# Rotating a matrix by 90 degrees: taller macro tiles, row chunks that come free one by one, and narrow macro tiles at both ends

## The chip, the cores and the metric

The kernel runs on one core of a Trainium2 chip. The metric is device time in microseconds (us), lower is better. The core has 16 DMA engines, a TensorE (PE), a VectorE (DVE), a ScalarE (ACT), and a sequencer (SP) that issues the reads here; ACT issues the writes.

## The reference

```python
def setup_inputs():
    return {"x": np.random.randn(8192, 8192).astype(np.float32), "k": 1}

def reference(x, k):
    return np.rot90(x, k)
```

There is no arithmetic to speak of: 268.4 MB are read, 268.4 MB are written. A rotation is a transpose with the order of the rows reversed.

## The kernel before

A macro tile is 512 rows by 4096 columns. Each 128-row strip is read as one DMA of 2 MB with runs of 16 KB (tile `a`), DVE copies it with every block of 128 columns reversed (`ar`), PE transposes 128x128 blocks into PSUM, ACT copies PSUM to an output tile of 1 MB (`o`), and ACT issues its write. A row of an output block is 512 floats, so each piece in memory is 2 KB.

```python
R = 512; C = 4096; RT = R // P; CG = C // P; G = 2048 // R; PW = 2048 // R
a_pool: bufs=2      r_pool: bufs=2 * RT      o_pool: bufs=5      psum: bufs=2
for r0 in range(0, N, R):
    for c0 in range(0, M, C):
        for t in range(RT):
            a = a_pool.tile([P, C], dt, tag="a")
            nc.sync.dma_start(out=a[:], in_=x[r0 + t * P : r0 + (t + 1) * P, c0 : c0 + C])
            ar = r_pool.tile([P, C], dt, tag="ar")
            nc.vector.tensor_copy(...)            # reversed within each 128 columns
        for g0 in range(0, CG, G):
            o = o_pool.tile([P, G, R], dt, tag="o")
            ...                                   # 16 transposes into ps, then:
            nc.scalar.copy(o[:, G - PW - h : G - h, :], ps[:])
            nc.scalar.dma_start(out=dst, in_=o[:])   # 128 x 4 pieces of 512 floats
```

## Time and profile before

Before: 1280.81 us median of 4 runs (1279.27 to 1282.25). Four lines of the page: DMA busy share and rate in 40 slices, and the two lines of the chain that ended last.

```profile
DMA  9999999999999999999999999999999999999998
GB/s 364 424 425 424 426 423 424 426 425 424 424 425 427 422 426 424 424 426 426 422 422 425 422 425 424 422 422 424 427 417 427 420 423 426 417 428 421 425 422 352
DMA 91%; PE 4%; ACT 3%; issue 0%; DVE 0%; ACTq 0%; SPq 0%
DMA out_dram<-o 90%; PE ps L96 4%; ACT o L101 3%; DMA a<-in_x_dram 2%; DVE ar L83 0%; ACTq L107 0%; ACTq L101 0%; SPq L77 0%
```

Between the ends the DMA engines are never idle: only their rate, and the two ends, can be improved. GB/s counts what is read and what is written together. The windows view gives, per stretch, its length, busy time of PE, PEld, DVE, ACT and POOL, the granted clock, the DMA busy share and GB/s.

```profile
0.00:170.00 170.00, 86.00 (x480) 76.57 (x480) 45.70 (x20) 53.39 (x29) 0.70 (x6) 0.73 1.00 414
170.00:1116.00 946.00, 535.31 (x3072) 486.56 (x3072) 215.82 (x95) 358.39 (x192) 0.00 (x0) 0.72 1.01 424
1116.00:1278.20 162.20, 86.74 (x544) 78.20 (x544) 29.64 (x13) 67.18 (x36) 0.00 (x0) 0.77 0.98 410
```

Two lines of the waits view, 170 to 1116 us (waiter <- releaser: us in total, times, longest):

```profile
ACT o L101 <- DMA out_dram<-o: 548.3, 159, 6.9
DVE ar L83 <- PE ps L96: 370.0, 25, 21.2
```

And the beginning, where only reads run (timeline: start us, duration, what; in brackets the idle time before and its releaser):

```profile
8.01 2.29 DVE L83 COPY ar<-a 128x4096 f32<-128x4096 f32 x1 [8.01 <-DMA a<-in_x_dram]
12.87 2.29 DVE L83 COPY ar<-a 128x4096 f32<-128x4096 f32 x1 [2.57 <-DMA a<-in_x_dram]
18.92 2.29 DVE L83 COPY ar<-a 128x4096 f32<-128x4096 f32 x1 [3.76 <-DMA a<-in_x_dram]
24.41 2.29 DVE L83 COPY ar<-a 128x4096 f32<-128x4096 f32 x1 [3.19 <-DMA a<-in_x_dram]
```

Strips of 2 MB come 4.9 us apart at first and then 5.5 to 6.1 us apart. With two `a` buffers at most two reads are in flight, and that is not enough to keep the rate when nothing is written beside them (tested in e8 and e13 below).

### The profile page before, as it was taken

How to read it: one execution, taken by the hardware profiler on the slowest of the kernel's cores; microseconds unless marked ns; L12 is line 12 of the kernel's file. 1: busy time of each engine (PE TensorE's matmuls, PEld its weight loads, DVE VectorE, ACT ScalarE, POOL GpSimd, SP SyncE). 2: the span in 40 equal slices, each digit the busy share in tenths (PEclk: the TensorE clock that was granted, in tenths of full speed). 3: DMA queues.
4: the chain of work that ended last, by engine and by line, in shares of the span. 5: the costliest groups of instructions: out<-in, count | busy, mean ns of one | idle time of the engine just before them, and what ended most of it. 6: DMA issues, size and time to landing. Idle time of an engine off the chain costs nothing.

```text
span 1278.2 us, 9636 instructions
## 1 busy us (share of the span) xinstructions
PE 708.0 (55%) x4096; PEld 641.3 (50%) x4096; DVE 291.2 (23%) x128; ACT 479.0 (37%) x257; POOL 0.7 (0%) x6
## 2 busy tenths in 40 slices
PE   2546565555545656546555465555565645656464
PEld 1545554455544545545554455554554534546453
DVE  3322222122221221212222122221222221222210
ACT  1324443343432434324343344342343432534354
POOL 0000000000000000000000000000000000000000
PEclk9757675777877777667686767777767776777788
DMA  9999999999999999999999999999999999999998
GB/s 364 424 425 424 426 423 424 426 425 424 424 425 427 422 426 424 424 426 426 422 422 425 422 425 424 422 422 424 427 417 427 420 423 426 417 428 421 425 422 352
DMA packets 55339, 537.51 MB, mean 421 GB/s; under 512 B 6144, under 2 KB 6144, under 8 KB 6144
## 3 DMA queue, kind: packets, MB, share of 16 engines
q10 hardware_dynamic: 36864, 268.45, 50.5%
q1 hardware_dynamic: 18432, 268.44, 49.6%
q8 instruction: 32, 0.52, 0.2%
q14 instruction: 11, 0.09, 0.0%
HBM read 268.44 MB, written 268.44 MB: 420 GB/s over the span
## 4 chain that ended last, share of the span: by engine, by line
DMA 91%; PE 4%; ACT 3%; issue 0%; DVE 0%; ACTq 0%; SPq 0%
DMA out_dram<-o 90%; PE ps L96 4%; ACT o L101 3%; DMA a<-in_x_dram 2%; DVE ar L83 0%; ACTq L107 0%; ACTq L101 0%; SPq L77 0%
## 5 line engine op out<-in xcount | busy, mean ns | idle before, releaser
L96 PE MATMUL ps<-ident,ar 128*128 128x128 f32 x4096 | 708.0, 348 | 557.2 <-ACT o L101 531.6
L96 PEld LDWEIGHTS ps<-ident,ar 128*128 128x128 f32 x4096 | 641.3, 183 | 623.5 <-ACT o L101 596.2
L101 ACT COPY o<-ps 128x2048 f32<-128x2048 f32 x256 | 477.7, 1868 | 787.4 <-DMA out_dram<-o 708.7
L83 DVE COPY ar<-a 128x4096 f32<-128x4096 f32 x128 | 291.2, 2293 | 943.6 <-DMA a<-in_x_dram 500.6
L101 ACT ACT_TABLE_LOAD x1 | 1.3, 1283 | 0.7 <-PEq L124 0.7
masks.py:199 POOL TENSOR_SCALAR_AFFINE_SELECT ident<-ident 128x128 f32<-128x128 f32 x1 | 0.3, 293 | 0.1
masks.py:197 POOL MEMSET ident<- 128x128 f32 x1 | 0.2, 204 | 0.3 <-POOLq L124 0.3
L124 POOL MEMSET const-bfloat16-1.0<- 128x1 bf16 x1 | 0.1, 101 | 0.0
L124 POOL MEMSET const-uint8-127<- 128x1 uint8 x1 | 0.1, 101 | 0.0
L124 POOL MEMSET const-float32-0.0<- 128x1 f32 x1 | 0.1, 98 | 0.2 <-issue 0.2
L124 POOL MEMSET const-float32-1.0<- 128x1 f32 x1 | 0.1, 98 | 0.0
## 6 DMA issues: line engine op xcount, KB each, us to landing
a<-in_x_dram SPq DMA_DIRECT2D x128, 2048.0 KB, 12.7
out_dram<-o ACTq DMA_DIRECT2D x256, 1024.0 KB, 20.9
```

Source lines behind the costliest of these rows:

```text
L83: nc.vector.tensor_copy(out=ar.rearrange("r (b m) -> r b m", m=P), in_=a.rearrange("r (b m) -> r b m", m=P)[:, :, ::-1],)
L96: nc.tensor.transpose(ps[:, PW - 1 - w, t * P : (t + 1) * P], rows[t][:, col : col + P], ident,)
L101: nc.scalar.copy(o[:, G - PW - h : G - h, :], ps[:])
L124: nc = _bacc.Bacc("TRN2", target_bir_lowering=False, num_devices=1)
```

## The change

The intent: output pieces of 4 KB (macro tiles of 1024 rows), packets of 16 KB in both directions (a packet is one entry of the profile's DMA records: what one engine moved in one go), row buffers cut into 512-column chunks that come free one by one so that one macro tile plus a little is enough, and narrow macro tiles at the beginning and end, so that the first write comes early and little is left after the last read.

```diff
-R = 512
-C = 4096
+R = 1024
+CH = 512
-G = 2048 // R          # 4
-PW = 2048 // R         # 4
+G = 4
+PW = 2
+def widths(first, last, M):
+    if first:
+        return [512, 512, 1024, 2048, 4096]
+    if last:
+        return [4096, 2048, 1024, 512, 512]
+    return [M // 2] * 2
-    r_pool bufs=2 * RT     # 8 strips of 16 KB per partition
-    o_pool bufs=5          # 1 MB each
+    r_pool bufs=68         # chunks of 2 KB per partition; a macro tile has 64
+    o_pool bufs=2          # 2 MB each
-        for c0 in range(0, M, C):
+        for C in widths(r0 == 0, r0 + R == N, M):
+                for j in range(C // CH):
+                    ar = r_pool.tile([P, CH // P, P], dt, tag="ar")
+                    nc.vector.tensor_copy(...)     # one chunk
+                    chunks[t, j] = ar
```

(The transposes read `chunks[t, j]`. One output group `g0` uses up column `j` of all 8 strips, and so releases 8 chunks.)

More of the change, by code (lines that the diff above doesn't have):

```diff
@@ L10 @@
 P = 128
-R = 512
-C = 4096
+R = 1024
 RT = R // P
-CG = C // P
-G = 2048 // R
-PW = 2048 // R
+CH = 512
+G = 4
+PW = 2
 def whole_reads(nc):
@@ L65 @@
     a_pool = ctx.enter_context(tc.tile_pool(name="a_pool", bufs=2))
-    r_pool = ctx.enter_context(tc.tile_pool(name="r_pool", bufs=2 * RT))
-    o_pool = ctx.enter_context(tc.tile_pool(name="o_pool", bufs=5))
+    r_pool = ctx.enter_context(tc.tile_pool(name="r_pool", bufs=68))
+    o_pool = ctx.enter_context(tc.tile_pool(name="o_pool", bufs=2))
     psum_pool = ctx.enter_context(
@@ L72 @@
     for r0 in range(0, N, R):
-        for c0 in range(0, M, C):
-            rows = []
+        c0 = 0
+        for C in widths(r0 == 0, r0 + R == N, M):
+            chunks = {}
             for t in range(RT):
@@ L79 @@
                 )
-                ar = r_pool.tile([P, C], dt, tag="ar")
-                nc.vector.tensor_copy(
-                    out=ar.rearrange("r (b m) -> r b m", m=P),
-                    in_=a.rearrange("r (b m) -> r b m", m=P)[:, :, ::-1],
-                )
-                rows.append(ar)
-            for g0 in range(0, CG, G):
+                for j in range(C // CH):
+                    ar = r_pool.tile([P, CH // P, P], dt, tag="ar")
+                    nc.vector.tensor_copy(
+                        out=ar[:],
+                        in_=a[:, j * CH : (j + 1) * CH].rearrange(
+                            "r (b m) -> r b m", m=P
+                        )[:, :, ::-1],
+                    )
+                    chunks[t, j] = ar
+            for g0 in range(0, C // P, G):
                 o = o_pool.tile([P, G, R], dt, tag="o")
@@ L93 @@
                     for w in range(PW):
-                        col = (g0 + h + w) * P
+                        g = g0 + h + w
                         for t in range(RT):
@@ L97 @@
                                 ps[:, PW - 1 - w, t * P : (t + 1) * P],
-                                rows[t][:, col : col + P],
+                                chunks[t, g * P // CH][:, g % (CH // P), :],
                                 ident,
@@ L107 @@
                 nc.scalar.dma_start(out=dst, in_=o[:])
+            c0 += C
 _INS = ['x', 'k']
```

## The prediction

> **What bounds the kernel now.** The 16 DMA engines. The page's slices show 420 to 428 GB/s nearly throughout; the windows view gives a DMA share of 1.00 to 1.02 from 40 to 1270 us; the chain of waits is 91% DMA. PE is busy 55%, ACT 37%, DVE 23%: their idle time costs nothing. 537 MB at 424 GB/s is 1267 of the 1278 us. The Trainium skill ("DMA: Bandwidth & Descriptors", Specifications) gives a fabric ceiling of 435 GB/s; the trace agrees (no 10 us above 433), so at most 3% is left.
>
> **Removed.** Output rows become pieces of 4 KB instead of 2 KB. In the DMA packet records a 16 KB read takes 0.612 us (mean 0.616), an 8 KB write packet (four 2 KB pieces) 0.314, so 16 KB written costs 0.629. Estimate: 0.616 to 0.620 after; over 16,384 packets on 16 engines that saves 9 to 13 us (DMA floor 1274 to 1264). A gain over 2% is nearly impossible.
>
> **Added.** Less work in flight. Now two macro tiles of rows are buffered and five 1 MB outputs, so writes never dry up (in no 1 us bin of the middle is their share under 0.18). After: 68 chunks, of which one macro tile takes 64, and two outputs of 2 MB.
> - Chunks are claimed row by row but released column by column: the next macro tile's row 2 is read only after group 3 is transposed, row 3 after group 7. So some rows are read while no writes run, and some writes run without reads.
> - Writes alone: a 2 MB output transfers in 4.95 us; refilling its buffer takes 0.43 (landing) + 2 x 1.94 (copies) + 0.55 (issue) + 0.9 to 1.3 (first packet) = 5.8 to 6.2 us. With two buffers DMA idles 0.4 to 0.6 us per 2 MB.
> - Reads alone, two 2 MB buffers: the head of the old kernel is this case. Its rows came 5.5 to 6.1 us apart (timeline: DVE at 12.87, 18.92, 24.41, 30.52) against 4.9 at full rate.
> Estimate: 2.5 to 6.5 us lost per macro tile of 79 us, 35 to 90 us in all.
> - Narrow tiles: reads of 256 KB with two buffers are bound by their round trip (issue 0.33, first packet 1.0, transfer 0.65, landing 0.4, copy 0.35 = 2.7 us, two in flight: 1.4 to 1.8 us each, 150 to 190 GB/s). The first write starts near 22 us instead of 33.6, but the first 80 us lose 16 to 32 us, against 5 now. The end loses 15 to 25 us, where the old tail wrote at 417 GB/s to its last packet.
>
> DVE's 1024 small copies (estimate 0.33 us each, 340 in all) and the unchanged PE and ACT work stay off the path, except within these round trips.
>
> **Sum.** 1278 - 10 + (35 to 90) + (25 to 45) = about 1330 to 1405; predicted 1370 us, 8 in 10 between 1310 and 1430. Faster by over 2%: 1%; within 2%: 7%; slower: 92%.
>
> **What would show it.** Write packets of 16 KB at 0.616 to 0.620 us; mean near 390 GB/s, lowest in the first two slices and the last; pure reading (350 to 390 GB/s) and pure writing (380 to 390) in turn; DVE waiting for PE at chunk reuse, ACT for outputs.
>
> **What would make it wrong.** If read-only stretches in mid kernel run at full rate (the slow head being a cold start), and small DMAs turn round faster than 2.7 us, the loss shrinks to about 30 us and the result is "same", 1300.

## The result, and the profile after

After: 1323.68 us median of 4 runs (1322.81 to 1323.85). Ratio 1.0334, interval 1.0316 to 1.0351: slower. (A ratio is the mean time of one kernel's fast runs over that of the other's in the same rounds, so it is not quite the ratio of the medians.) The time lies inside the predicted range, but the loss against the old kernel is 43 us where about 90 was forecast, and it is not where the prediction put most of it. The same page lines of the changed kernel:

```profile
DMA  6899999999999999999999999999999999999788
GB/s 220 292 378 429 389 425 426 429 430 429 429 429 427 431 428 425 426 429 428 430 429 429 427 429 427 424 427 427 429 430 428 426 426 426 425 401 348 287 352 338
DMA 83%; DVE 12%; issue 2%; ACT 1%; PE 1%; DVEq 0%; ACTq 0%; SPq 0%
```

The same three stretches, by the windows view of the changed kernel:

```profile
0.00:170.00 170.00, 66.71 (x352) 52.89 (x352) 52.15 (x144) 37.95 (x21) 0.70 (x6) 0.68 0.88 344
170.00:1160.00 990.00, 580.88 (x3217) 553.85 (x3218) 280.43 (x808) 367.17 (x202) 0.00 (x0) 0.74 1.01 428
1160.00:1321.90 161.90, 85.95 (x529) 81.75 (x527) 27.17 (x72) 61.91 (x34) 0.00 (x0) 0.74 0.87 343
```

The middle became faster than it was (428 against 424 GB/s); everything is lost at the two ends. From here on, the *loss* of a stretch is its length less the time its bytes would take at 428 GB/s, worked out from the packet records of the kernel's own reads and writes in the one profiled execution. Beginning (first 170 us), middle, end (last 162 us):

| | beginning | middle | end | sum |
|---|---|---|---|---|
| before | 6.2 | 10.8 | 6.8 | 23.8 |
| after | 33.9 | 1.8 | 31.8 | 67.5 |

The difference, 43.7 us, is the difference of the spans (1321.9 and 1278.2). The page's first slices show the beginning at 220 and 292 GB/s. Its timeline:

```profile
3.33 0.43 DVE L93 COPY ar<-a 128x512 f32<-128x512 f32 x1 [3.33 <-DMA a<-in_x_dram]
3.95 0.43 DVE L93 COPY ar<-a 128x512 f32<-128x512 f32 x1 [0.19 <-DMA a<-in_x_dram]
6.37 0.43 DVE L93 COPY ar<-a 128x512 f32<-128x512 f32 x1 [1.99 <-DMA a<-in_x_dram]
7.04 0.43 DVE L93 COPY ar<-a 128x512 f32<-128x512 f32 x1 [0.24 <-DMA a<-in_x_dram]
...
22.28 0.43 DVE L93 COPY ar<-a 128x512 f32<-128x512 f32 x1 [0.53 <-DMA a<-in_x_dram]
28.77 0.43 DVE L93 COPY ar<-a 128x512 f32<-128x512 f32 x1 [6.06 <-DMA a<-in_x_dram]
```

Strips of 256 KB come in pairs, a pair per 3.0 us: two buffers, and a buffer is asked to take a new strip only when its last one has landed and been copied. That is 175 GB/s at best (157 to 161 counted over 10 us). From 21.3 us the first output is being written, and after the copy at 22.28 us no strip lands for 6 us.

In the middle, two waits and a piece of the timeline (170 to 1160 us, and around 610 us):

```profile
DVE ar L93 <- DMA a<-in_x_dram: 710.8, 101, 8.5
ACT o L113 <- DMA out_dram<-o: 629.8, 101, 11.9
```

```profile
607.61 0.55 ACTq L119 DMA_DIRECT2D out_dram<-o  x1
607.70 2.78 DVE L93 COPY ar<-a 128x512 f32<-128x512 f32 x8 [6.99 <-DMA a<-in_x_dram]
...
617.38 0.55 ACTq L119 DMA_DIRECT2D out_dram<-o  x1
617.45 2.78 DVE L93 COPY ar<-a 128x512 f32<-128x512 f32 x8 [6.97 <-DMA a<-in_x_dram]
```

DVE waits for reads 101 times and ACT for outputs 101 times, always both within one period of 9.8 us: one strip read (2 MB) for one output written (2 MB). DVE never waits for PE here (0.2 us in the whole run), where the old kernel's DVE did so for 370 us of its middle. The packet records agree: 2.1 to 2.2 MB each way in every 10 us but the first. The old kernel moved 2.8 MB in and 1.4 MB out for 20 to 50 us, and then mostly wrote.

### The profile page after: what moved, and what is told of

It reads as the page before. It is cut to its first block, busy times and chain, and to the rows that moved or that the text cites. A ratio compares the mean times of both kernels' runs of the same rounds, so it can differ in the third digit from the quotient of the medians.

```text
span 1321.9 us, 10544 instructions
## 1 busy us (share of the span) xinstructions
PE 733.6 (55%) x4096; PEld 688.5 (52%) x4096; DVE 359.8 (27%) x1024; ACT 467.0 (35%) x257; POOL 0.7 (0%) x6
## 4 chain that ended last, share of the span: by engine, by line
DMA 83%; DVE 12%; issue 2%; ACT 1%; PE 1%; DVEq 0%; ACTq 0%; SPq 0%
DMA a<-in_x_dram 81%; DVE ar L93 12%; DMA out_dram<-o 2%; ACT o L113 1%; PE ps L108 1%; DVEq L93 0%; ACTq L119 0%; SPq L86 0%; ACTq L113 0%
## 5 line engine op out<-in xcount | busy, mean ns | idle before, releaser
L108 PE MATMUL ps<-ident,ar 128*128 128x128 f32 x4096 | 733.6, 360 | 578.4 <-ACT o L113 494.2
L108 PEld LDWEIGHTS ps<-ident,ar 128*128 128x128 f32 x4096 | 688.5, 193 | 623.2 <-ACT o L113 525.1
L113 ACT COPY o<-ps 128x2048 f32<-128x2048 f32 x256 | 465.7, 1869 | 846.6 <-DMA out_dram<-o 677.2
L93 DVE COPY ar<-a 128x512 f32<-128x512 f32 x1024 | 359.8, 423 | 928.1 <-DMA a<-in_x_dram 927.7
```

What stands on the lines that cost most here:

```text
L93: nc.vector.tensor_copy(out=ar[:], in_=a[:, j * CH : (j + 1) * CH].rearrange("r (b m) -> r b m", m=P)[:, :, ::-1],)
L108: nc.tensor.transpose(ps[:, PW - 1 - w, t * P : (t + 1) * P], chunks[t, g * P // CH][:, g % (CH // P), :], ident,)
```

## The experiments

Thirteen kernels ran, all with correct results. Times are medians; ratios are to the kernel before, run in the same rounds; losses as above. By a bound of 2%, e5, e6, e10 and e11 are slower than the kernel before and all others count as the same; smaller differences are read from the intervals and the traces.

| run | us | ratio (95%) | beginning | middle | end |
|---|---|---|---|---|---|
| e1 wide tiles only | 1279.34 | 0.9981 (0.9965-0.9998) | 8.3 | 1.4 | 10.6 |
| e2 narrow at the beginning | 1303.09 | 1.0175 (1.0158-1.0192) | 33.7 | 1.7 | 10.9 |
| e3 narrow at the end | 1301.34 | 1.0156 (1.0141-1.0171) | 11.1 | 2.0 | 31.7 |
| e4 narrow, read in 2 MB | 1283.64 | 1.0020 (1.0005-1.0035) | 18.2 | 1.3 | 10.2 |
| e5 fixed circle of chunks | 1457.76 | 1.1341 (1.1287-1.1394) | 25.3 | 146.3 | 29.3 |
| e6 2 KB pieces | 1321.79 | 1.0323 (1.0281-1.0365) | 15.7 | 31.9 | 12.5 |
| e7 outputs 4 x 1 MB | 1289.25 | 1.0062 (1.0042-1.0081) | 12.6 | 13.6 | 7.6 |
| e8 e7, reads 4 x 1 MB | 1278.80 | 0.9980 (0.9964-0.9996) | 3.6 | 6.4 | 12.2 |
| e9 old, 16 KB packets | 1279.22 | 0.9983 (0.9969-0.9997) | 7.9 | 7.1 | 7.8 |
| e10 one shared pool | 1428.06 | 1.1153 (1.1136-1.1171) | 22.5 | 125.2 | 22.6 |
| e11 e10, narrow at the end | 1449.12 | 1.1315 (1.1296-1.1333) | 22.5 | 125.8 | 44.3 |
| e12 e8, narrow at the end | 1280.60 | 0.9993 (0.9981-1.0006) | 3.6 | 8.4 | 12.9 |
| e13 borrowed buffers | 1270.51 | 0.9918 (0.9905-0.9932) | 3.2 | 1.2 | 9.9 |

e1 and e3, which have the same code at the beginning, differ there by 2.8 us. Five kernels begin with the same reads into two buffers (e1, e3, e5, e6, e7), and their first write leaves at 56.7 us in e1 and at 59.4 to 60.7 us in the others. So single differences of 3 or 4 us in that column decide nothing.

### e1, e2, e3: which end, and is it the narrow tiles?

The theory was that the narrow tiles cost all that is lost; the rival, that tall macro tiles with two output buffers lose at the ends whatever their width.

```diff
 def widths(first, last, M):
-    if first: ...        # e1 and e3
-    if last: ...         # e1 and e2
     return [M // 2] * 2
```

> Undo only the narrow macro tiles: all sixteen are 1024 by 4096. Theory (the narrow tiles cost it): the loss of the changed kernel lies in its first 170 us (33.9 us against a rate of 428 GB/s) and its last 162 us (31.8 us), while 170 to 1160 us loses 1.8 us; with wide tiles the head becomes the old kernel's (reads alone, rows 5.5 to 6 us apart, loss 8 to 10 us) and the end eight outputs written alone (5.4 to 5.6 us each, loss 8 to 14 us): 1270 to 1290 us. Rival (taller macro tiles and two outputs of 2 MB cost it, wherever nothing else runs beside them): over 1300 us, with most of the loss still in head and tail.

> Narrow macro tiles only at the beginning. Theory: the wide kernel's time plus 20 to 28 us (head loss 34 instead of 8 to 10), so 1293 to 1312, and this plus the one with narrow tiles only at the end, less the wide one, gives the changed kernel's 1323 within 5 us. Rival (the end alone costs it): within 5 us of the wide one.

> Narrow macro tiles only at the end. Theory: the wide kernel's time plus 15 to 24 us, so 1288 to 1310. Rival (the beginning alone costs it): within 5 us of the wide one.

The windows view of e1:

```profile
0.00:170.00 170.00, 74.28 (x426) 68.22 (x427) 56.12 (x162) 48.16 (x27) 0.70 (x6) 0.85 0.98 408
170.00:1112.70 942.70, 552.75 (x3069) 529.96 (x3068) 267.44 (x772) 349.00 (x193) 0.00 (x0) 0.74 1.01 428
1112.70:1274.70 162.00, 94.90 (x605) 90.17 (x603) 31.64 (x92) 69.95 (x39) 0.00 (x0) 0.78 0.94 399
```

The theory holds. Without narrow tiles the kernel is about as fast as the old one; each narrow end costs 22 to 24 us, and they add: 1303.1 + 1301.3 - 1279.3 = 1325.1 against 1323.7 measured. The first write of e1 leaves at 56.7 us instead of 21.3, and it does not matter: the engines were reading meanwhile.

### e4: is it the small reads?

```diff
-                a = a_pool.tile([P, C], dt, tag="a")
-                nc.sync.dma_start(out=a[:], in_=x[r0 + t * P : r0 + (t + 1) * P, c0 : c0 + C])
+                n = min(RT, 4096 // C)
+                if t % n == 0:
+                    an = a_pool.tile([P, n, C], dt, tag="a")
+                    nc.sync.dma_start(out=an[:], in_=x[r0 + t * P : r0 + (t + n) * P, c0 : c0 + C]
+                                      .rearrange("(n p) c -> p n c", p=P))
+                a = an[:, t % n, :]
```

> Narrow macro tiles at both ends as changed, but rows of a narrow tile are read together in one DMA of 2 MB (8 rows of 512, 4 of 1024, 2 of 2048) into the same two buffers. Theory (the round trip of small reads with two in flight is the cost): the first 512-wide tile lands at about 7 to 9 us instead of 19, head loss falls to 8 to 15 us, end loss to 10 to 18, total 1275 to 1298. Rival (2 KB descriptors, or the order narrow-wide itself, where a tile twice as wide must be read while its predecessor is written): still over 1305.

```profile
0.00:170.00 170.00, 66.90 (x394) 56.99 (x395) 53.36 (x154) 45.22 (x25) 0.70 (x6) 0.71 0.96 383
170.00:1122.00 952.00, 559.84 (x3101) 534.59 (x3100) 269.72 (x779) 351.56 (x194) 0.00 (x0) 0.74 1.01 428
1122.00:1284.00 162.00, 92.65 (x606) 87.92 (x603) 32.25 (x94) 70.47 (x39) 0.00 (x0) 0.80 0.97 401
```

With the same two buffers, the same narrow tiles and the same short runs in memory, larger reads take away 40 of the 43 us: the round trip of small reads, two in flight, was the cost. The 2 KB runs were not: a 2 KB read packet takes 0.084 us (median), and an eighth of a 16 KB one is 0.076 us; with the 4 and 8 KB packets reckoned in the same way that is under 2 us at each end. The end comes down to that of the wide kernel (10.2 against 10.6). The beginning misses its expectation (18.2, expected 8 to 15; the first tile landed at 9.5 us, expected 7 to 9), and stays worse than with wide tiles (8.3). There the rival has a share: in the packet records nothing is written from 40 to 50, 70 to 80 and 130 to 140 us (293, 364 and 406 GB/s), while a tile twice as wide as the one just written is read.

### e5: the step of the prediction that failed

The prediction took the 68 chunk buffers for a circle. The pool gives any buffer that is free: the eight copies in a row after every output, shown above, are not possible in a circle of 68, where they would need buffers that later groups release. In this run the circle is forced:

```diff
-    r_pool bufs=68
+    r_pool bufs=1
-                    ar = r_pool.tile([P, CH // P, P], dt, tag="ar")
+                    ar = r_pool.tile([P, CH // P, P], dt, tag=f"ar{made % 68}")
+                    made += 1
```

> The wide kernel with the 68 chunk buffers claimed in a fixed circle (chunk n always takes buffer n modulo 68) instead of any buffer that is free. This is what the prediction silently assumed. If its arithmetic was sound and only this assumption was false: reads of rows 3 to 7 of the next macro tile cluster after the last group, DMA idles 2.5 to 6.5 us per macro tile, DVE waits for PE return by some hundred us, and the time is 1310 to 1370 us. If the arithmetic too was false: within 15 us of the wide kernel (1279).

A line of the windows and one of the waits, both for the middle of e5:

```profile
170.00:1293.20 1123.20, 478.56 (x3172) 424.97 (x3169) 277.30 (x788) 363.60 (x199) 0.00 (x0) 0.70 0.94 373
```

```profile
DVE ar L91 <- PE ps L106: 248.1, 44, 10.6
```

The waits of DVE for PE come back, reads and writes run in turn (in the packet records, 395 to 420 us is reading alone, at 1.4 to 2.1 MB per 5 us, and 425 to 440 us is writing alone), and the middle loses 146 us. So the order of claiming and releasing did decide it, and the assumption was the false step. The arithmetic on top of it was too low by a factor of about two or more: this middle moves the bytes of 12.5 macro tiles, so 146 us are 12 us for each, where 2.5 to 6.5 had been estimated, and the total is above the expected 1310 to 1370.

### e6, e7, e8, e9: what made the middle faster?

The prediction credited the 4 KB piece alone. The other thing that changed is the size of a write packet, 8 KB before and 16 KB now. The Trainium skill ("DMA: Bandwidth & Descriptors", Queues, rings and completion order) says that a DMA engine takes the queues in turn, one whole packet at a time. The traces agree: with 16 KB reads against 8 KB writes the old kernel moves 2.8 MB in and 1.4 MB out per 10 us while both have work; with 16 KB both ways it is 1 to 1. (An exception, reads that have just been asked for, comes up under "Why" below.)

e6 halves the pieces, by two DMAs per output:

```diff
-                o = o_pool.tile([P, G, R], dt, tag="o")
+                o = o_pool.tile([P, 2, G, R // 2], dt, tag="o")
-                nc.scalar.dma_start(out=dst, in_=o[:])
+                for u in range(2):
+                    nc.scalar.dma_start(out=dst_of_half_u, in_=o[:, u])
```

> The wide kernel with each output tile written as two DMAs of 2 KB pieces (packets of 8 KB, as in the old kernel). Theory (the gain in the middle is the 4 KB piece): the middle falls from 427.4 to about 423 GB/s, write packets return to 0.314 us per 8 KB, and the time rises by 8 to 13 us to 1287 to 1293. Rival (the gain in the middle is the lockstep of one row read per output written): the middle stays at 427 and the time within 4 us of the wide kernel.

It is a miss for both theories: the middle lost 31.9 us. The edit halves pieces and packets together, so it cannot tell the two apart; DVE waited 501.5 us for PE in the middle. e7 keeps the 4 KB pieces and halves the packets:

```diff
-G = 4
+G = 2
-    o_pool bufs=2
+    o_pool bufs=4
```

> The wide kernel with four output buffers of 1 MB instead of two of 2 MB. Theory (writes alone idle DMA because two buffers cannot cover landing, copies and issue): after the last read the outputs leave at over 405 GB/s instead of 350, end loss 10.6 falls to 5 to 7 us, time 1271 to 1276. Rival (the end is bound by ACT copies at 1.87 us per MB or by PE): no change at the end.

Middle of e7, windows and waits:

```profile
170.00:1126.20 956.20, 546.77 (x3081) 501.88 (x3080) 273.99 (x769) 358.30 (x192) 0.00 (x0) 0.73 1.01 422
```

```profile
DVE ar L89 <- PE ps L104: 415.9, 95, 9.1
```

The end improved a little less than expected (7.6, expected 5 to 7; 381 GB/s after the last read instead of 350, expected over 405), but the middle lost 12 us more than in e1, which the expectation had not foreseen, and the total is a miss. With unequal packets the reads run ahead (1.5 MB against 0.6 in some 5 us), use up the chunks, and DVE waits for PE. How that costs time is argued, not shown: the DMA share stays at 1.01 in e6 and e7. What their records do show is more long packets: what the middle's packets took beyond their medians sums to 14 us per engine in e7 and 24 in e6, against 3 in e1. Why e6 loses more than e7 stays open. e8 makes the packets equal again at 8 KB:

```diff
+AW = 2048
-    a_pool bufs=2
+    a_pool bufs=4
+                for b in range(0, C, AW):
+                    a = a_pool.tile([P, AW], dt, tag="a")      # half a strip, 1 MB
```

> As the run before, and rows read in halves of 1 MB (8 KB pieces) into four buffers instead of two of 2 MB. Theory (reads alone lose time for want of DMAs in flight): rate before the first write rises from 369 to 385 to 410 GB/s, head loss 8.3 falls to 4 to 6, and the time to 1267 to 1273, the best so far and below the old kernel by 0.6 to 1.1%. Rival (reads alone are slow while the chip is cold, whatever is in flight): the head stays near 369 GB/s and the time within 2 us of the run before.

The beginning behaves as expected (402 GB/s before the first write instead of 369, loss 3.6), and the middle recovers to 426. Four buffers of 1 MB hold no more bytes than two of 2 MB: what differs is that three quarters of them, and not half, can be in flight while one is emptied. The total misses the expectation: the end lost 12.2, and 8 KB packets are a little dearer than 16 KB ones (reads: 2 x 0.309 us against 0.611).

e9 separates piece from packet in the old kernel: 16 KB write packets made of eight 2 KB pieces.

```diff
-G = 2048 // R
+G = 8
-    o_pool bufs=5
+    o_pool bufs=2
```

> The old kernel (512 rows, two macro tiles of rows buffered) with output tiles of eight row blocks in two buffers instead of four in five: a write packet becomes 16 KB in eight pieces of 2 KB, as large as a read packet. If the piece of 2 KB is what cost the old kernel its middle (423.1 GB/s against 427.4): packets of about 0.627 us and a middle at 423 again. If the packet of 8 KB beside reads of 16 KB cost it (one packet of each queue in turn, so reads run ahead at 2 to 1): packets of 0.615 us, and reads and writes close to 1 to 1 in every 10 us, middle at 427. The total may be 1272 to 1290, as two outputs leave gaps at the end.

```profile
170.00:1115.30 945.30, 554.21 (x3065) 531.69 (x3066) 219.74 (x96) 348.81 (x192) 0.00 (x0) 0.74 1.01 425
```

Reads and writes went 1 to 1 and DVE stopped waiting for PE, as in the changed kernel, but the rate rose only part of the way. Writing 16 KB takes, by the medians of the packet records, 0.628 us as two 8 KB packets of four 2 KB pieces (old), 0.624 as one packet of eight 2 KB pieces (e9), 0.618 as two 8 KB packets of two 4 KB pieces (e7) and 0.615 as one of four 4 KB pieces (e1). Over 1,024 times 16 KB per engine that is 3 to 4 us for the packet and 9 to 10 us for the piece. The loss of the middle fell in the same order: 10.8 (old), 7.1 (e9), 1.4 (e1). So the prediction was right about the gain in the main, but credited to the piece alone what the packet shares in; equal packets also set the mix of reads and writes, and that matters where few buffers are spare, as e7 shows.

### e10, e11, e12: attempts at better ends

e10 drew strips and outputs from one pool of four buffers; e11 is e10 with narrow tiles at the end only, read in 2 MB; e12 is e8 with narrow tiles at the end, read in 1 MB.

```diff
-    a_pool bufs=2
-    o_pool bufs=2
+    a_pool bufs=4                                         # e10, e11
-                o = o_pool.tile([P, G, R], dt, tag="o")
+                o = a_pool.tile([P, G, R], dt, tag="a")
```

> The wide kernel with row buffers and output buffers drawn from one pool of four 16 KB slots, so that up to four reads are in flight before the first write and up to four writes after the last read; packets stay 16 KB both ways. Theory (head and end lack DMAs in flight): head loss 8 falls to about 3, end loss 10.6 to about 6, middle at 427, time 1266 to 1272. Rival (a pool shared by both sides breaks the one read for one write of the middle): middle under 424 GB/s, time over 1280.

> As the run before, with narrow macro tiles at the end only, their rows read in DMAs of 2 MB. If narrow tiles at the end do what they were meant to (writes of a wider tile still pending while a narrow one is read, so no gap between the last read and its first write): end loss 3 to 6, 2 to 4 us below the run before. If not: equal or slower by up to 10 us.

> The kernel with four 1 MB buffers on each side, and narrow macro tiles at the end read in DMAs of 1 MB. Its end without them shows a dip to 310 to 327 GB/s for 20 us after the last wide tile was read. If narrow tiles fill that dip: end loss 12.2 falls to 5 to 8 us and the time from 1279 to 1271 to 1275. If their small pieces cost as much as they save: 1277 to 1283.

The middle of e10:

```profile
170.00:1262.80 1092.80, 419.86 (x3078) 359.25 (x3078) 273.19 (x788) 349.17 (x192) 0.00 (x0) 0.69 0.90 379
```

For e10 the rival was right, by far: the two sides take all four buffers in turn. In the packet records 390 to 396 us is reading alone, then nothing moves until 405, then 30 us are writing alone; the middle falls to 379 GB/s. With the middle in that state e11 says only that its narrow end was worse still (44.3 against 22.6). e12 gained nothing: its narrow tiles did not fill the dip but brought one of their own (234 GB/s from 1210 to 1220 us, nearly all of it reads in 2 KB packets).

### e13: more transfers in flight at the ends alone

What was still open was whether the rest of the loss at the ends is a lack of transfers in flight. e7 and e8 had raised their number, but had changed packets too. e13 leaves packets and middle alone: in the beginning the output buffers are idle, at the end the row buffers are.

```diff
-                a = a_pool.tile([P, C], dt, tag="a")
+                if r0 == c0 == 0 and t % 2 == 1:
+                    a = o_pool.tile([P, C], dt, tag="o")
+                else:
+                    a = a_pool.tile([P, C], dt, tag="a")
-                o = o_pool.tile([P, G, R], dt, tag="o")
+                if r0 + R == N and c0 + C == M and (g0 // G) % 2 == 1:
+                    o = a_pool.tile([P, G, R], dt, tag="a")
+                else:
+                    o = o_pool.tile([P, G, R], dt, tag="o")
```

(Applied to the wide kernel, e1.)

> The wide kernel, but every second row of the first macro tile is read into an output buffer (idle until the first write), and every second output of the last macro tile uses a row buffer (idle after the last read): four transfers of 2 MB in flight at both ends, packets of 16 KB and the middle unchanged. If transfers in flight are the cause: rate before the first write 369 to 400 or more, head loss 8.3 to 3 to 4, end loss 10.6 to 6 to 7 (the gap between the last read and its first write stays), middle at 427, time 1267 to 1272, 0.7 to 1.1% below the old kernel. If the ends are bound otherwise (cold reads; ACT copies of 1.87 us per MB): head and end losses as in the wide kernel, 1276 to 1281.

Windows of e13, and the beginning of its timeline:

```profile
0.00:170.00 170.00, 80.28 (x448) 73.59 (x448) 58.23 (x168) 49.25 (x28) 0.70 (x6) 0.82 1.00 421
170.00:1106.70 936.70, 538.51 (x3045) 509.97 (x3046) 263.39 (x760) 347.91 (x192) 0.00 (x0) 0.73 1.01 428
1106.70:1268.70 162.00, 91.78 (x605) 86.37 (x603) 33.28 (x96) 69.95 (x39) 0.00 (x0) 0.78 0.95 402
```

```profile
12.93 2.77 DVE L92 COPY ar<-a 128x512 f32<-128x512 f32 x8 [2.11 <-DMA a<-in_x_dram]
17.83 2.77 DVE L92 COPY ar<-a 128x512 f32<-128x512 f32 x8 [2.13 <-DMA a<-in_x_dram]
22.72 2.77 DVE L92 COPY ar<-a 128x512 f32<-128x512 f32 x8 [2.12 <-DMA a<-in_x_dram]
27.61 2.77 DVE L92 COPY ar<-a 128x512 f32<-128x512 f32 x8 [2.12 <-DMA a<-in_x_dram]
```

Strips now land 4.9 us apart from the start, so the slow reads of the old beginning were not a cold chip but two reads in flight instead of four. (In e10, with four slots for them, the first seven strips came 4.9 us apart too.) This is the best kernel, 0.8% below the old one. The end improved less than expected (9.9, expected 6 to 7): once going, writes leave at 416 to 419 GB/s, but from 1220 to 1230 us only 251 GB/s move. The last strip is copied from 1218.07 us, and its first output, which needs that strip, is issued at 1224.87 us. That gap stays open to improvement.

## Why the prediction was right or wrong

- **Right: what bounds the kernel, and the gain.** The middle lost 10.8 us before and 1.8 after; 9 to 13 had been predicted, all of it for the piece, where e9 gives the packet a share. Write packets: median 0.615 us (predicted 0.616 to 0.620), mean 0.624.
- **Wrong: "the next macro tile's row 2 is read only after group 3 is transposed, row 3 after group 7"**, and from it 35 to 90 us lost in the middle. Chunks are indeed claimed row by row and released column by column, but a claim is not tied to one buffer. Measured: 1.8 us. A group releases 8 chunks, a strip needs 8, and since any free buffer will do, each group written lets in exactly one strip. The kernel settles into one strip read per output written, with reads beside every write, so neither side ever runs alone. e5 shows that the predicted pattern appears when the circle is forced. "Pure reading and pure writing in turn" and "DVE waiting for PE at chunk reuse" were the signs named; neither was there (0.2 us).
- **Right in mechanism, undersized: the narrow tiles.** 25 to 45 us predicted for both ends. Measured: 33.9 + 31.8 less the old kernel's 6.2 + 6.8, which is 52.7 us. Of these the narrow tiles themselves account for 46.8 (against the wide kernel e1, 8.3 + 10.6), and the other 5.9 are the ends of the wide kernel. The rate of the narrow reads was right (157 to 161 GB/s, predicted 150 to 190), and so was the first write (21.3 us, predicted 22). The first 80 us lost 28 us (277 GB/s on average), within the predicted 16 to 32; what was missed is another 6 us up to 170 us, where wider tiles are read alone, and the end, 31.8 (15 to 25). The round trip was a little longer than said, 3.0 us for 2.7. One thing was not counted. In the packet records, the reads asked for at 21.78 and 22.74 us send no packet until 25.98 us, while 1.75 MB of the first output are written. Turns by packet would have given such reads one byte for eight written, so they are not the explanation. The same delay shows in e10, where reads begin again while writes run: 3.9 to 4.3 us from the issue to the first packet in all 15 cases, against 1.0 us at the start of the kernel. What holds these reads back stays open.
- **Right in part: reads alone with two buffers.** The old head was rightly read as a limit of two transfers in flight (e8, e13); it just does not occur in the middle.
- **The sum.** 43.7 = 52.7 - 9.0. Predicted +92: the middle's term was a loss that never came. Without it the prediction's own terms give 1293 to 1313, so that 1324 lay within 1310 to 1430 is partly luck: the ends cost more than was said.

## What to carry to other kernels

In a kernel that only moves data, as here, an early first write is worth nothing if the engines are busy reading. What counts at the ends is that enough is in flight while a buffer is emptied and asked for again: four transfers kept the rate where two of the same size (e13), or of the same bytes in all (e8), did not. So a tile made narrow must keep its DMAs large, or the buffers of the idle side can be lent to the busy one. Before costing buffer reuse, find out whether the pool hands out any free buffer or a fixed circle: here that was the difference between losing 1.4 us and 146 us in the middle. Where reads and writes share the engines, give both the same packet size if few buffers are spare, so that each write lets in one read.

## What the Trainium skill lacked or had wrong

- "DMA: Bandwidth & Descriptors", Bandwidth: it advises DMAs of 1 MiB or more, but not how many must be in flight. Here reads of 2 MB alone ran at 340 to 369 GB/s up to the first write with two in flight (before, e1, e3, e5 to e7), and at 407 with four (e13; 429 to 432 from 10 to 40 us); 256 KB with two in flight gave 157 to 161.
- "DMA: Bandwidth & Descriptors", SWDGE vs HWDGE vs iDMA: for SWDGE it gives a packet as at most 4096 bytes preferably, and says nothing of HWDGE. The packets recorded here for DMAs issued by SP and ACT are as long as the contiguous run on the source side (2 to 16 KB), and 16 KB ones were the fastest (428 GB/s in the middle).
- The same page, Queues, rings and completion order: that the queues take turns by packet agrees with the runs while both queues have work; it does not say what follows, that unequal packets make one side run ahead (2.8 MB read for 1.4 MB written per 10 us), nor that reads asked for while only writes run can wait about 4 us for their first packet (3.9 to 4.3 us in e10, 4.2 in the changed kernel).
- The same page, Specifications: the ceiling of 435 GB/s agrees with the runs; 428 GB/s, reads and writes together, were held for 937 to 990 us. Its 358 GB/s per core for HBM does not bind a core that runs alone, as "HBM Reference", Specifications (TRN2), says.
- No page has the cost of a shorter destination piece within a 16 KB packet, 0.615 us for four of 4 KB and 0.624 for eight of 2 KB (medians); "DMA: Bandwidth & Descriptors", Why small descriptors are slow, has a fixed overhead per packet with an example of 256 bytes, and no time for pieces of this size.
